# A decoder trunk on one core: seven row tiles of the first gate summed on VectorE, the squares added there, and the norm's steps spread over the last units

## The chip, the cores and the metric

The kernel runs on one core of a Trainium2 chip. The core has TensorE (PE, matrix products, with a queue of its own for loading weights, PEld), VectorE (DVE), ScalarE (ACT), GpSimd (POOL) and SyncE (SP), which issues the transfers that 16 DMA engines carry out. The metric is the device time of one execution in microseconds (us). The kernel before took 1970.44 us, the median of 3 runs (1969.87 to 1972.51).

## What is computed

A trunk of two layers on 256 tokens of width 2048, all in float32. Cut to what matters here:

```
sc = silu(c)
shift_m, scale_m, gate_m, shift_f, scale_f, gate_f = split(sc @ mod_w[0] + mod_b[0], 6)   # six vectors of 2048
h = rmsnorm(x, norm_mix[0]) * (1 + scale_m) + shift_m
x = x + gate_m * pool_mixer(h, pool_w[0], pool_scale[0])          # causal means over 2, 4, 8, 16 tokens, then a product per group
h = rmsnorm(x, norm_ffn[0]) * (1 + scale_f) + shift_f
x = x + gate_f * swiglu(h, ffn_gate[0], ffn_up[0], ffn_down[0])
...                                                               # layer 1: latent attention on shared keys and values, then its own swiglu
return rmsnorm(x, final_norm)
```

Each of the six vectors is a product of one row (sc) with a 2048 x 2048 block of `mod_w`, 16 MB that are read once. The pooling mixer of layer 0 needs the first three vectors, the feed-forward part behind it the next two.

## The kernel before

The front of the kernel (up to the first matrix product of layer 0's feed-forward part) is written in an order by hand: inside `tc.manual_schedule()` each engine executes its instructions in the order in which the code gives them. It is a list of 56 units. Units 0 to 15 stream the weights of `shift_m`, 16 to 31 those of `scale_m`, 32 to 47 those of `gate_m`, one row tile (128 rows x 2048) each, 1 MB; units 48 to 55 (the "block") stream the first 512 columns of `shift_f` and `scale_f`, two row tiles each, also 1 MB. Behind unit n the functions that `then(n, ...)` has put down are called, for one n in the order in which they were put down.

A unit (class `Strips`, line 240) loads its tile into one of six `raw` buffers, through SP's queue, and `use` (line 255) multiplies it on PE: `s_strip` holds silu(c) in the first of 32 columns for each row tile, so that four matmuls of 512 columns write to four strips of 32 partitions of one PSUM bank, over which the units of one vector add up. A float32 matmul is two instructions, so a unit has eight. Behind the last unit of a vector, `columns` (line 265) copies the bank with ACT and turns it with small matmuls (line 273) into columns; `with_bias` (line 783) adds the bias on DVE.

Layer 0's mixer works on turned data, `xT`, 16 tiles of 128 x 256. `pool_modulate` (line 828) applies scale and shift to a group of four tiles (line 832 on ACT, line 834 on DVE), `pool_product` (line 842) computes a quarter of a group on PE and, for each second quarter, copies the result with ACT (line 848). `mix_in` (line 852) adds the gated result to `xT` on DVE (line 856) and squares it on ACT (line 861). `mix_total` (line 864) sums the squares over the 128 partitions with matmuls of one column, 16 instructions per group of four tiles, all into one PSUM tile `total`. `norm_total` (line 878) makes the root mean square from it (line 456 on DVE, line 457 on POOL), spreads it over the partitions by a diagonal matrix (line 884 on DVE) and a matmul (line 886), and copies it to `rstd_b` with ACT (line 887). `turn_back` (line 871) turns a group of `xT` back with eight PE transposes (line 875) and two DVE copies (line 876), for the residual stream. `hidden_T` (line 889) scales a group by `rstd_b` on DVE (line 894), `halves_T` (line 898) applies scale and shift and splits the result in two parts (lines 903 to 905), which the feed-forward part multiplies.

The feed-forward part (line 433) splits each weight tile of 1 MB into two parts, one copied by ACT (line 409), the rest subtracted by DVE (line 411). `w_early` loads and splits its first tile ahead of its turn. Beside it, the vectors of later use are summed in the background on DVE (lines 235 and 293), into accumulators of the tag `acc`, which has two buffers; `front`, the tile that holds `s_strip`, the biases and the gate's columns, is one of these.

In the kernel before, behind unit 31 + g follows `pool_modulate(g)`; behind units 32 to 47 one quarter of the pool product each; behind unit 47 `mix_in` of all four groups; behind unit 48 + g `mix_total(g)`; behind unit 51 + g `turn_back(g)`; behind unit 51 `norm_total`, behind 52 `hidden_T(0)`, behind 53 `w_early`.

Of the kernel before, what the change touches and what calls it, by code (L numbers as in the profile page):

```python
# [17 lines left out]
P = 128  # L18
# [82 lines left out]
def tile_trunk(ctx: ExitStack, tc: tile.TileContext, a: dict, out: bass.AP):  # L101
# [9 lines left out]
    def nm(s):  # L111
        n_names[0] += 1
        return f"{s}_{n_names[0]}"
# [10 lines left out]
    def t2k(shape, dt=F32):  # L124
        return work.tile(shape, dt, tag="t2k", bufs=7, name=nm("t2k"))

    def small(shape, dt=F32, bufs=4):
        return work.tile(shape, dt, tag="sm", bufs=bufs, name=nm("sm"))
# [4 lines left out]
    def ps_t():  # L133
        return psum.tile([P, CH], F32, tag="ps", name=nm("ps"))
# [53 lines left out]
    pool.memset(mhalf, -0.5)  # L188


    front = work.tile([P, KD * (STRIP + 7)], F32, tag="acc", bufs=2, name="front")
    s_strip = front[:, :KD * STRIP].rearrange("p (k m) -> p k m", m=STRIP)
    bcol = front[:, KD * STRIP:KD * (STRIP + 5)].rearrange("p (i k) -> p i k", k=KD)
    gm_col, ps_col = (front[:, KD * (STRIP + i):KD * (STRIP + i + 1)] for i in (5, 6))
    pool.memset(front[:, :KD * STRIP], 0.0)
    cps = ps_t()
    pe.transpose(cps[:, :KD], crow, ident[:KD, :KD])
    s_col = const.tile([P, KD], F32, name="s_col")
# [19 lines left out]
    class Part:  # L218
        def __init__(self, w, b, done):
            self.w, self.b, self.done, self.kt = w, b, done, 0  # L220
# [17 lines left out]


    class Strips:  # L240
        def __init__(self, i, pair, done):
            self.n, self.rows, self.done, self.kt = (2, 2, done, 0) if pair else (NSTRIP, 1, done, 0)
            w = a["mod_w"][0][:, i * D:(i + self.rows) * D]
            self.w = w.rearrange("(k p) (i n) -> p k i n", p=P, i=2)[:, :, :, :CH] if pair else                 w.rearrange("(k p) (i n) -> p k i n", p=P, i=NSTRIP)
# [8 lines left out]
            self.use(self.load())  # L253

        def use(self, r):
            if self.kt == 0:
                self.bank = ps_t()
            for m in range(NSTRIP):
                k, i = m // self.n, m % self.n
                pe.matmul(self.bank[m * STRIP:(m + 1) * STRIP, :], lhsT=s_strip[:, self.kt + k, :], rhs=r[:, k, i, :],  # L260
                          start=self.kt == 0, stop=self.kt + self.rows == KD)
            self.kt += self.rows
            if self.kt == KD:
                self.done(self.columns())

        def columns(self):

# [157 lines left out]
    def w_early(src):  # L425
        early[repr(src)] = w_unit(src)
# [27 lines left out]
    def rsqrt_mean(dst, ss, n):  # L454
        v = small([P, NT])
        dve.tensor_scalar(out=v, in0=ss, scalar1=1.0 / n, scalar2=EPS, op0=ALU.mult, op1=ALU.add)
        pool.tensor_tensor(out=dst, in0=v, in1=mhalf, op=ALU.pow)
# [117 lines left out]
    def ffn_weights(l):  # L575
        return a["ffn_gate"][l], a["ffn_up"][l], a["ffn_down"][l]
# [202 lines left out]
    def with_bias(dst, v, i, factor=None):  # L779

        kt = slice(0, v.shape[1] * KL)
        col = lambda t_: t_[:, kt].rearrange("p (i b) -> p i b", b=KL)
        dve.tensor_tensor(out=col(dst), in0=v, in1=col(bcol[:, i]), op=ALU.add)  # L783
        if factor is not None:
            dve.tensor_tensor(out=col(dst), in0=col(dst), in1=col(factor), op=ALU.mult)
# [4 lines left out]

    shift = Strips(0, False, lambda v: with_bias(cols[:, C_SM0, :], v, 0))
    scale = Strips(1, False, lambda v: with_bias(cols[:, C_AM0, :], v, 1, vcol[:, V_NM:V_NM + KD]))
    gate = Strips(2, False, lambda v: with_bias(gm_col, v, 2, ps_col))
    block = Strips(3, True, block_cols)


# [50 lines left out]
        if n % 2 == 1:  # L847
            act.activation(ysum[g // 2][:, g % 2, n - 1:n + 1, :], mixed[g], AF.Copy)

    squares, total = {}, ps_t()  # L850

    def mix_in(g):

        for k in range(KL):
            kt = g * KL + k
            dve.scalar_tensor_tensor(out=xT[:, kt, :], in0=ysum[g // 2][:, g % 2, k, :], scalar=gm_col[:, kt:kt + 1],
                                     in1=xT[:, kt, :], op0=ALU.mult, op1=ALU.add)
        squares[g] = []
        for h2 in range(2):
            sq = t2k([P, 2, T])  # L860
            act.activation(sq, xT[:, g * KL + 2 * h2:g * KL + 2 * h2 + 2, :], AF.Square)
            squares[g].append(sq)

    def mix_total(g):
        for k in range(KL):
            for tok in range(NT):
                pe.matmul(total[:, tok:tok + 1], lhsT=squares[g][k // 2][:, k % 2, tok * P:(tok + 1) * P], rhs=ones[:, 0:1],
                          start=g + k + tok == 0, stop=g == ND - 1 and k == KL - 1 and tok == NT - 1)


    def turn_back(g):
# [3 lines left out]
                pe.transpose(pt[:, k * P:(k + 1) * P], xT[:, g * KL + k, tok * P:(tok + 1) * P], ident)  # L875
            dve.tensor_copy(back[tok][:, g * CH:(g + 1) * CH], pt)

    def norm_total():

        r = small([P, NT])  # L880
        rsqrt_mean(r, total[:, :NT], D)
        diag = t2k([P, NT, P])
        for tok in range(NT):
            dve.tensor_scalar(out=diag[:, tok, :], in0=ident, scalar1=r[:, tok:tok + 1], scalar2=None, op0=ALU.mult)
        pt = ps_t()
        pe.matmul(pt[:, :T], lhsT=ones, rhs=diag.rearrange("p t q -> p (t q)"), start=True, stop=True)
        act.activation(rstd_b, pt[:, :T], AF.Copy)

    def hidden_T(j):
        parts = []  # L890
        for k in range(KL):
            if k % 2 == 0:
                both = t2k([P, 2, T])
            dve.tensor_tensor(out=both[:, k % 2, :], in0=xT[:, j * KL + k, :], in1=rstd_b, op=ALU.mult)
            parts.append(both[:, k % 2, :])
        return parts
# [14 lines left out]
    def then(n, f, *args):  # L911
        after.setdefault(n, []).append((f, args))
# [7 lines left out]
    then(16, rope_tables)  # L920
    for g in range(ND):
        then(n_mix - 8 + 2 * g, load_pool_w, g)
        then(n_mix - 1 + g, pool_modulate, g)
        for q in range(4):
            then(n_mix + 4 * g + q, pool_product, g, q)
        then(n_block - 1, mix_in, g)
        then(n_block + g, mix_total, g)
        then(n_block + 3 + g, turn_back, g)
    then(n_block + 3, norm_total)
    then(n_block + 4, lambda: first.append(hidden_T(0)))  # L930
    then(n_block + 5, lambda: w_early(ffn_weights(0)[GATE][0:CH, 0:CH]))

    with tc.manual_schedule():
        flat_all = hl_t([P, len(WINDOWS), T], F32)
        pool_all = [act_t([P, 2, KL, T], F32) for _ in range(2)]
        back = [t_.rearrange("p g k t -> p (g k t)") for t_ in pool_all]
        stat_start()
        for tok in range(NT):
            for j in range(ND):
                stat_piece(tok, j, xn[tok])  # L940
        rstd = stat_finish()
        for n, part in enumerate(units):
            if n < len(ahead):
                part.use(ahead[n])
            else:
                part.unit()
            for f, args in after.get(n, ()):
                f(*args)
        first = halves_T(0, first[0])
# [302 lines left out]
```

## Time and profile before

| | |
|---|---|
| median of 3 runs | 1970.44 us (1969.87 to 1972.51) |
| the profiled execution | 1972.76 us, span from first to last instruction 1971.0 us |
| busy share of the span | PE 96%, PEld 78%, DVE 73%, ACT 43%, POOL 2% |
| mean granted TensorE clock | 0.978 of full speed |
| first matmul of the feed-forward part (line 433) | 192.01 us after the span's start |

All times in the profile count from the span's start. A row of the timeline merges neighbouring instructions of one line: start, duration, engine, line, operation, out<-in, count, and in brackets how long the engine was idle before it and what ended this. TensorE's clock is either full (2.4 GHz, shown as 1.00) or half (1.2 GHz, 0.50); a value between is a stretch in which it changed.

### The profile page before, as it was taken

To read this page: it belongs to the slowest core of one execution; us is meant where nothing else is said; L and a number is where in the kernel's file an instruction comes from. 1 tells how busy PE (TensorE), PEld (TensorE's weight loads), DVE (VectorE), ACT (ScalarE), POOL (GpSimd) and SP (SyncE) were. 2 spreads that over 40 slices of the span, in tenths; PEclk is the share of its full clock that TensorE was granted. 3 is DMA by queue.
4 is the path that set the end of the run, shared out by engine and by line. 5 is a ranking of instruction groups with operands and counts; after the bars stand their busy time and mean duration, and the time that the engine had idled before them with its cause. 6 is when DMAs were issued, how large, how long until landed. Compare 5 with 4: busy or idle time off the path is not lost. (4 is left out here: it accounts for less than half of the span.)

```text
span 1971.0 us, 22348 instructions
## 1 busy us (share of the span) xinstructions
PE 1895.6 (96%) x8949; PEld 1532.0 (78%) x8949; DVE 1442.2 (73%) x1298; ACT 843.0 (43%) x915; POOL 30.1 (2%) x30
## 2 busy tenths in 40 slices
PE   6698999999999999999899999999999999999998
PEld 3145788888888888887788987888888888888886
DVE  1114989999778778888989985889987556554556
ACT  3023444444533333334675744544444433343333
POOL 0000000000000000000000000000000000000000
PEclk9787999999999999999899999999999999999999
DMA  9997999998998989988788684989977667665661
GB/s 395 412 404 277 350 342 336 316 322 314 341 335 299 329 311 332 335 332 313 277 317 308 217 306 136 355 304 325 313 279 259 231 235 256 235 203 187 195 221 70
DMA packets 225441, 572.73 MB, mean 291 GB/s; under 512 B 11997, under 2 KB 16421, under 8 KB 203571
## 3 DMA queue, kind: packets, MB, share of 16 engines
q1 hardware_dynamic: 225338, 571.31, 81.1%
q8 instruction: 70, 1.15, 0.2%
q14 instruction: 33, 0.27, 0.0%
HBM read 564.98 MB, written 6.29 MB: 290 GB/s over the span
## 5 line engine op out<-in xcount | busy, mean ns | idle before, releaser
L433 PE MATMUL ps<-hl,act 128*128 128x512 f32 x7008 | 1610.9, 391 | 6.2 <-ACT hl L409 2.7
L433 PEld LDWEIGHTS ps<-hl,act 128*128 128x128 f32 x7008 | 1317.1, 189 | 282.1 <-ACT hl L409 3.6
L411 DVE TENSOR_TENSOR hl<-raw,hl 128x2048 fp32r<-128x2048 f32 x296 | 676.3, 2288 | 244.1 <-ACT hl L409 239.8
L409 ACT ACTIVATE hl<-raw 128x2048 fp32r<-128x2048 f32 x296 | 566.5, 1917 | 666.3 <-PE ps L433 595.0
L235 DVE SCALAR_TENSOR_TENSOR acc<-raw,s_col,acc 128x2048 f32<-128x2048 f32 x112 | 262.6, 2345 | 1.2 <-DMA raw<-in_mod_w_dram 1.0
L293 DVE SCALAR_TENSOR_TENSOR acc<-raw,s_col,acc 128x1024 f32<-128x1024 f32 x112 | 143.3, 1279 | 2.1 <-DMA raw<-in_mod_w_dram 0.8
L260 PE MATMUL ps<-raw,front 128*32 128x512 f32 x448 | 74.0, 749 | 26.3 <-DMA raw<-in_mod_w_dram 26.2
L600 DVE TENSOR_TENSOR act<-ps,act 128x512 f32<-128x512 f32 x96 | 64.0, 685 | 10.6 <-PE ps L433 10.3
L260 PEld LDWEIGHTS ps<-raw,front 128*32 128x32 f32 x448 | 10.4, 121 | 61.2 <-DMA raw<-in_mod_w_dram 46.3
L669 DVE TENSOR_TENSOR x<-ps,x 128x512 f32<-128x512 f32 x32 | 22.1, 690 | 33.6 <-PE ps L433 33.6
L634 ACT ACTIVATE act<-ps 128x512 fp32r<-128x512 f32 x44 | 23.6, 593 | 40.0 <-PE ps L631 36.6
L452 ACT ACTIVATE junk<-x 128x512 bf16<-128x512 f32 x24 | 15.1, 628 | 59.9 <-DVE x L550 39.7
L678 ACT ACTIVATE t2k<-ps 128x512 f32<-128x512 f32 x24 | 14.2, 591 | 56.6 <-PE ps L433 56.6
L1050 PE MATMUL ps<-act,hl 128*128 128x256 f32 x128 | 37.2, 291 | 0.5 <-DVE hl L411 0.5
L845 PEld LDWEIGHTS ps<-act,act 128*128 128x128 f32 x128 | 24.1, 198 | 16.3 <-issue 12.6
L1051 PE MATMUL ps<-act,hl 128*128 128x256 f32 x128 | 36.7, 287 | 0.0
L783 DVE TENSOR_TENSOR cols<-ps,front 128x16 f32<-128x16 f32 (+1 forms) x4 | 0.6, 166 | 49.3 <-PE ps L273 49.2
L1052 PE MATMUL ps<-act,hl 128*128 128x256 f32 x128 | 36.1, 286 | 0.0
L682 DVE TENSOR_TENSOR t2k<-ps,t2k 128x512 f32<-128x512 f32 x24 | 16.6, 690 | 25.7 <-PE ps L433 25.7
L845 PE MATMUL ps<-act,act 128*128 128x256 f32 x128 | 33.7, 408 | 0.0
L598 ACT ACTIVATE act<-ps 128x512 f32<-128x512 f32 x32 | 19.0, 596 | 26.9 <-PE ps L433 26.8
L500 ACT ACTIVATE t2k<-ps,cols 128x256 f32<-128x256 f32 x48 | 24.8, 569 | 12.4 <-PE ps L486 11.8
(188 smaller groups left out, 981.6 us busy)
## 6 DMA issues: line engine op xcount, KB each, us to landing
raw<-in_mod_w_dram SPq DMA_DIRECT2D x128, 1024.0 KB, 7.3
raw<-in_ffn_gate_dram SPq DMA_DIRECT2D x88, 1024.0 KB, 7.3
raw<-in_ffn_up_dram SPq DMA_DIRECT2D x88, 1024.0 KB, 5.2
raw<-in_ffn_down_dram SPq DMA_DIRECT2D x88, 1024.0 KB, 5.2
raw<-in_mod_w_dram SPq DMA_DIRECT2D x128, 512.0 KB, 5.8
raw<-in_kv_mod_w_dram SPq DMA_DIRECT2D x32, 1024.0 KB, 7.1
raw<-in_w_o_dram SPq DMA_DIRECT2D x16, 1024.0 KB, 5.2
raw<-in_w_uq_dram SPq DMA_DIRECT2D x8, 768.0 KB, 6.3
```

The costliest lines, as they stand in the source:

```text
L235: dve.scalar_tensor_tensor(out=self.acc, in0=r, scalar=s_col[:, self.kt:self.kt + 1], in1=self.acc, op0=ALU.mult, op1=ALU.add)
L260: pe.matmul(self.bank[m * STRIP:(m + 1) * STRIP, :], lhsT=s_strip[:, self.kt + k, :], rhs=r[:, k, i, :], start=self.kt == 0, stop=self.kt ...
L293: dve.scalar_tensor_tensor(out=self.acc, in0=r[:, k], scalar=s_col[:, self.kt + k:self.kt + k + 1], in1=self.acc, op0=ALU.mult, op1=ALU.add)
L409: hi_ins = act.activation(hi, r, AF.Copy)
L411: lo_ins = dve.tensor_tensor(out=lo, in0=r, in1=hi.bitcast(F32), op=ALU.subtract)
L433: pe.matmul(banks[tok], lhsT=t_[:, i, k, tok * P:(tok + 1) * P], rhs=w[:, k, :], start=first and n < len(part), stop=last and n >= len(ord ...
L500: act.activation(full, pts[k // 2][:, k % 2, :], AF.Identity, scale=scale, bias=bias)
L600: dve.tensor_tensor(out=part, in0=banks[tok], in1=part, op=ALU.add)
L845: pe.matmul(mixed[g][:, n % 2, :], lhsT=wp[g][:, k, ns], rhs=pool_all[g // 2][:, g % 2, k, :], start=k == 0, stop=k == KL - 1)
L1050: pe.matmul(pt[:, h, :], lhsT=wl(h0 + h, k), rhs=t_[:, 0, k, :], start=k == 0, stop=False)
L1051: pe.matmul(pt[:, h, :], lhsT=wh(h0 + h, k), rhs=t_[:, 0, k, :], start=False, stop=False)
L1052: pe.matmul(pt[:, h, :], lhsT=wh(h0 + h, k), rhs=t_[:, 1, k, :], start=False, stop=k == KL - 1)
```

## The change

Units 32, 34, 36, 38, 40, 42 and 44, the even row tiles 0 to 12 of the gate, are multiplied by silu(c) and summed on DVE into an accumulator of the tag `acc` in place of PE's strips. Behind the strips of unit 47, the accumulator goes through the strips once, with a column of ones in place of silu(c). `pool_modulate` of groups 1 to 3 moves to units 33, 36 and 39, each quarter of the pool product by one unit (33 to 48). `mix_in` of groups 0 to 2 stays behind unit 47, that of group 3 goes behind unit 48. The squares are added on DVE over the row tiles, an add one half group behind its square, into one tile of two rows of tiles; `norm_sums` behind unit 51 sums it over the partitions with four matmuls and makes the diagonal. `turn_back(g)` moves to unit 49 + g, the spread of the norm and `hidden_T(0)` to unit 53, `w_early` to unit 52. Four tiles of the norm are allocated ahead of unit 47.

```diff
+    front = work.tile([P, KD * (STRIP + 7) + STRIP], F32, tag="acc", bufs=2, name="front")
+    one_strip = front[:, KD * (STRIP + 7):]
...
+    pool.memset(one_strip, 0.0)
+    pool.memset(one_strip[:, 0:1], 1.0)
...
         def use(self, r):
-            if self.kt == 0:
+            last = self.kt + self.rows == KD
+            if self.kt in self.aside:
+                s_ = s_col[:, self.kt:self.kt + 1]
+                if self.acc is None:
+                    self.acc = work.tile([P, 1, NSTRIP, CH], F32, tag="acc", bufs=2, name=nm("acc"))
+                    dve.tensor_scalar(out=self.acc, in0=r, scalar1=s_, scalar2=None, op0=ALU.mult)
+                else:
+                    dve.scalar_tensor_tensor(out=self.acc, in0=r, scalar=s_, in1=self.acc, op0=ALU.mult, op1=ALU.add)
+            else:
+                self.sum(lambda k: s_strip[:, self.kt + k, :], r, last and self.acc is None)
+            if last and self.acc is not None:
+                self.sum(lambda k: one_strip, self.acc, True)
+            self.kt += self.rows
+            if self.kt == KD:
+                self.done(self.columns())
+
+        def sum(self, weights, r, last):
+            first = self.bank is None
+            if first:
                 self.bank = ps_t()
             for m in range(NSTRIP):
                 k, i = m // self.n, m % self.n
-                pe.matmul(self.bank[m * STRIP:(m + 1) * STRIP, :], lhsT=s_strip[:, self.kt + k, :], rhs=r[:, k, i, :],
-                          start=self.kt == 0, stop=self.kt + self.rows == KD)
-            self.kt += self.rows
-            if self.kt == KD:
-                self.done(self.columns())
+                pe.matmul(self.bank[m * STRIP:(m + 1) * STRIP, :], lhsT=weights(k), rhs=r[:, k, i, :], start=first, stop=last)
...
-    gate = Strips(2, False, lambda v: with_bias(gm_col, v, 2, ps_col))
+    gate = Strips(2, False, lambda v: with_bias(gm_col, v, 2, ps_col), range(0, KD - 2, 2))
...
     def mix_in(g):
 
-        for k in range(KL):
-            kt = g * KL + k
-            dve.scalar_tensor_tensor(out=xT[:, kt, :], in0=ysum[g // 2][:, g % 2, k, :], scalar=gm_col[:, kt:kt + 1],
-                                     in1=xT[:, kt, :], op0=ALU.mult, op1=ALU.add)
-        squares[g] = []
         for h2 in range(2):
-            sq = t2k([P, 2, T])
-            act.activation(sq, xT[:, g * KL + 2 * h2:g * KL + 2 * h2 + 2, :], AF.Square)
-            squares[g].append(sq)
-
-    def mix_total(g):
-        for k in range(KL):
-            for tok in range(NT):
-                pe.matmul(total[:, tok:tok + 1], lhsT=squares[g][k // 2][:, k % 2, tok * P:(tok + 1) * P], rhs=ones[:, 0:1],
-                          start=g + k + tok == 0, stop=g == ND - 1 and k == KL - 1 and tok == NT - 1)
+            for k in range(2 * h2, 2 * h2 + 2):
+                kt = g * KL + k
+                dve.scalar_tensor_tensor(out=xT[:, kt, :], in0=ysum[g // 2][:, g % 2, k, :], scalar=gm_col[:, kt:kt + 1],
+                                         in1=xT[:, kt, :], op0=ALU.mult, op1=ALU.add)
+            pair = xT[:, g * KL + 2 * h2:g * KL + 2 * h2 + 2, :]
+            if g + h2 == 0:
+                act.activation(squares, pair, AF.Square)
+            else:
+                sq = t2k([P, 2, T])
+                act.activation(sq, pair, AF.Square)
+                late.append(lambda sq=sq: dve.tensor_tensor(out=squares, in0=squares, in1=sq, op=ALU.add))
+                if len(late) > 1:
+                    late.pop(0)()
+
+    late = []
+
+    def norm_sums():
+        late.pop()()
+        for tok in range(NT):
+            for k in range(2):
+                pe.matmul(total[:, tok:tok + 1], lhsT=squares[:, k, tok * P:(tok + 1) * P], rhs=ones[:, 0:1],
+                          start=tok + k == 0, stop=tok + k == 2)
+        rsqrt_mean(rstd_x1, total[:, :NT], D)
+        for tok in range(NT):
+            dve.tensor_scalar(out=diag[:, tok, :], in0=ident, scalar1=rstd_x1[:, tok:tok + 1], scalar2=None, op0=ALU.mult)
...
+    def norm_spread():
+
+        pe.matmul(total[:, T:], lhsT=ones, rhs=diag.rearrange("p t q -> p (t q)"), start=True, stop=True)
+        act.activation(rstd_b, total[:, T:], AF.Copy)
...
-        then(n_mix - 1 + g, pool_modulate, g)
+        then(n_mix - 1 + 3 * g - (g > 0), pool_modulate, g)
         for q in range(4):
-            then(n_mix + 4 * g + q, pool_product, g, q)
-        then(n_block - 1, mix_in, g)
-        then(n_block + g, mix_total, g)
-        then(n_block + 3 + g, turn_back, g)
-    then(n_block + 3, norm_total)
-    then(n_block + 4, lambda: first.append(hidden_T(0)))
-    then(n_block + 5, lambda: w_early(ffn_weights(0)[GATE][0:CH, 0:CH]))
+            then(n_mix + 1 + 4 * g + q, pool_product, g, q)
+        then(n_block - (g < ND - 1), mix_in, g)
+        then(n_block + 1 + g, turn_back, g)
+    then(n_block + 3, norm_sums)
+    then(n_block + 5, norm_spread)
+    then(n_block + 5, lambda: first.append(hidden_T(0)))
+    then(n_block + 4, lambda: w_early(ffn_weights(0)[GATE][0:CH, 0:CH]))
...
+            if n == n_block - 1:
+                squares, diag, total, rstd_x1 = t2k([P, 2, T]), t2k([P, NT, P]), ps_t(), small([P, NT])
```

## Rows read from the trace of the kernel before

**Rows 1.** The page's first part: busy us, share of the span, instructions.

```profile
PE 1895.6 (96%) x8949; PEld 1532.0 (78%) x8949; DVE 1442.2 (73%) x1298; ACT 843.0 (43%) x915; POOL 30.1 (2%) x30
```

**Rows 2.** Windows of 10 us: busy of each engine, granted clock, DMA share, GB/s.

```profile
120.00:130.00 10.00, 10.00 (x58) 5.17 (x58) 1.50 (x4) 2.17 (x5) 0.00 (x0) 1.00 1.01 416
...
150.00:160.00 10.00, 9.28 (x56) 5.68 (x56) 2.00 (x7) 1.83 (x3) 0.00 (x0) 1.00 1.01 360
...
210.00:220.00 10.00, 10.00 (x46) 8.26 (x45) 9.96 (x8) 6.01 (x6) 0.53 (x1) 1.00 0.98 336
```

**Rows 3.** Timeline of 100 to 135, PE: the gate's units.

```profile
104.05 1.93 PE L260 MATMUL ps<-raw,front 128*32 128x512 f32 x8 [3.23 <-DMA raw<-in_mod_w_dram]
...
110.36 3.78 PE L845 MATMUL ps<-act,act 128*128 128x256 f32 x8
...
120.01 1.07 PE L260 MATMUL ps<-raw,front 128*32 128x512 f32 x8
...
121.00 1.99 PE L845 MATMUL ps<-act,act 128*128 128x256 f32 x8
...
122.93 1.07 PE L260 MATMUL ps<-raw,front 128*32 128x512 f32 x8
```

**Rows 4.** Timeline of 155 to 182: the gate's end, mixing and the norm.

```profile
155.05 1.07 PE L260 MATMUL ps<-raw,front 128*32 128x512 f32 x8
...
158.14 0.18 DVE L785 TENSOR_TENSOR front<-front 128x16 f32<-128x16 f32 x1
158.35 5.63 DVE L856 SCALAR_TENSOR_TENSOR x<-act,front,x 128x256 f32<-128x256 f32 x14
...
172.55 1.97 PE L875 MATMUL ps<-con,x 128*128 128x128 f32 x8
...
177.76 0.16 DVE L456 TENSOR_SCALAR sm<-ps 128x2 f32<-128x2 f32 x1 [2.51 <-PE ps L867]
...
178.74 0.48 DVE L884 TENSOR_SCALAR t2k<-con,sm 128x128 f32<-128x128 f32 x2 [0.82 <-POOL sm L457]
...
179.37 1.19 PE L886 MATMUL ps<-t2k,ones 128*128 128x256 f32 x2 [1.64 <-DVE t2k L884]
...
180.49 1.94 PE L260 MATMUL ps<-raw,front 128*32 128x512 f32 x8
```

**Rows 5.** Timeline of 182 to 215: the front's end.

```profile
183.15 1.29 DVE L876 COPY act<-ps 128x512 f32<-128x512 f32 x2 [3.92 <-PE ps L875]
...
184.35 1.42 DVE L894 TENSOR_TENSOR t2k<-x,krT 128x256 f32<-128x256 f32 x4
...
186.49 1.09 PE L875 MATMUL ps<-con,x 128*128 128x128 f32 x8
...
186.89 2.28 DVE L411 TENSOR_TENSOR hl<-raw,hl 128x2048 fp32r<-128x2048 f32 x1
...
187.51 1.06 PE L260 MATMUL ps<-raw,front 128*32 128x512 f32 x8
...
192.01 0.73 PE L433 MATMUL ps<-hl,act 128*128 128x512 f32 x2 [1.60 <-ACT act L904]
```

**Rows 6.** Groups by line, 100 to 196: count, busy us, mean ns, idle before.

```profile
L867 PE MATMUL ps<-ones,t2k 128*128 128x1 f32 x64 | 10.9, 300 | 0.0
...
L834 DVE SCALAR_TENSOR_TENSOR act<-act,cols,t2k 128x256 f32<-128x256 f32 x16 | 6.5, 479 | 6.0 <-ACT t2k L832 5.9
```

**Rows 7.** Windows of 1 us in which the clock changed.

```profile
165.00:166.00 1.00, 1.00 (x9) 0.53 (x12) 0.31 (x1) 0.57 (x1) 0.00 (x0) 0.76 1.05 377
...
182.00:183.00 1.00, 1.00 (x9) 0.65 (x6) 0.00 (x0) 0.78 (x1) 0.00 (x0) 0.70 0.00 0
```

**Rows 8.** The page's parts 5 and 6: VectorE's sums; the units' loads.

```profile
L235 DVE SCALAR_TENSOR_TENSOR acc<-raw,s_col,acc 128x2048 f32<-128x2048 f32 x112 | 262.6, 2345 | 1.2 <-DMA raw<-in_mod_w_dram 1.0
...
raw<-in_mod_w_dram SPq DMA_DIRECT2D x128, 1024.0 KB, 7.3
```

**Rows 9.** The chain that ended last: start, us, engine, line.

```profile
1962.55 0.70 DVE x L550
```

More of the change, by code (lines that the diff above doesn't have):

```diff
@@ L188, in tile_trunk @@
     pool.memset(mhalf, -0.5)
-    front = work.tile([P, KD * (STRIP + 7)], F32, tag="acc", bufs=2, name="front")
+    front = work.tile([P, KD * (STRIP + 7) + STRIP], F32, tag="acc", bufs=2, name="front")
     s_strip = front[:, :KD * STRIP].rearrange("p (k m) -> p k m", m=STRIP)
+    one_strip = front[:, KD * (STRIP + 7):]
     bcol = front[:, KD * STRIP:KD * (STRIP + 5)].rearrange("p (i k) -> p i k", k=KD)
@@ L240, in tile_trunk, with __init__ @@
     class Strips:
-        def __init__(self, i, pair, done):
+        def __init__(self, i, pair, done, aside=()):
+            self.aside, self.acc, self.bank = aside, None, None
             self.n, self.rows, self.done, self.kt = (2, 2, done, 0) if pair else (NSTRIP, 1, done, 0)
@@ L848, in pool_product @@
             act.activation(ysum[g // 2][:, g % 2, n - 1:n + 1, :], mixed[g], AF.Copy)
-    squares, total = {}, ps_t()
     def mix_in(g):
-        for k in range(KL):
-            kt = g * KL + k
-            dve.scalar_tensor_tensor(out=xT[:, kt, :], in0=ysum[g // 2][:, g % 2, k, :], scalar=gm_col[:, kt:kt + 1],
-                                     in1=xT[:, kt, :], op0=ALU.mult, op1=ALU.add)
-        squares[g] = []
-        for h2 in range(2):
-            sq = t2k([P, 2, T])
-            act.activation(sq, xT[:, g * KL + 2 * h2:g * KL + 2 * h2 + 2, :], AF.Square)
-            squares[g].append(sq)
-    def mix_total(g):
-        for k in range(KL):
-            for tok in range(NT):
-                pe.matmul(total[:, tok:tok + 1], lhsT=squares[g][k // 2][:, k % 2, tok * P:(tok + 1) * P], rhs=ones[:, 0:1],
-                          start=g + k + tok == 0, stop=g == ND - 1 and k == KL - 1 and tok == NT - 1)
+        for h2 in range(2):
+            for k in range(2 * h2, 2 * h2 + 2):
[21 more added lines that the diff above has]
+            dve.tensor_scalar(out=diag[:, tok, :], in0=ident, scalar1=rstd_x1[:, tok:tok + 1], scalar2=None, op0=ALU.mult)
     def turn_back(g):
@@ L876, in turn_back @@
             dve.tensor_copy(back[tok][:, g * CH:(g + 1) * CH], pt)
[L878 to L887, printed above, removed]
+    def norm_spread():
+        pe.matmul(total[:, T:], lhsT=ones, rhs=diag.rearrange("p t q -> p (t q)"), start=True, stop=True)
+        act.activation(rstd_b, total[:, T:], AF.Copy)
     def hidden_T(j):
```

## The prediction, put down before the kernel was run

> **What bounds the kernel now.** TensorE (PE) is busy for 96% of the span [rows 1], and in the feed-forward part it is full: 46 matmuls of 512 columns in 10 us, 10.00 us busy at 210:220 [rows 2]. So the time after the first of these matmuls (line 433, at 192.01 [rows 5]) is taken as fixed, and the change is worth what it moves that start by. Before it lies the front: 56 units of 1 MB each that SP loads into six `raw` buffers.
>
> I read three views of the front. The windows first: at 120:130 the DMA moves 416 GB/s at a full share, so a unit (1.049 MB) lands every 2.52 us; at 150:160, with the block's smaller pieces, 360 GB/s [rows 2], between 2.8 and 2.9 us a unit. The PE timeline of the gate's units next: strips start at 120.01 and again at 122.93 [rows 3]. That is 2.92 us a unit, 0.40 more than the load: a quarter of the pool product (1.99) and the strips (1.07) overlap only slightly. PE is the bound there, and the buffers fill. Unit 31 is used at 104.05 as it lands [rows 3]; at the load's pace unit 47 would land at 104.05 + 16 x 2.52 = 144.4, but its strips start at 155.05 [rows 4]. Last the tail: from the end of those strips (156.1) to line 433 it takes 35.9 us. The row sums of the squares alone take 10.9 us of PE (64 instructions, line 867 [rows 6]), then PE waits for the norm chain (177.76 to 179.37 [rows 4]), all at a clock that had fallen from full to half in 165:166 and came back in 182:183 [rows 7]. So the front has two places where PE, not the load, decides.
>
> **The change part by part.**
>
> *Gate on VectorE (DVE).* Units 32, 34, ... 44 no longer issue strips; one more pass over the accumulator is added at unit 47. PE per pair of units becomes 2 x 1.98 + 0.94 (a strip pass beside a quarter, 2.92 - 1.98) = 4.9 us against 5.04 for two loads: balanced. Working: unit 33 lands at 109.1; its strips at half clock take 1.93 (at 104.05 [rows 3]), the quarter 3.78 (at 110.36 [rows 3]), to 114.8. Then 13 quarters (units 34 to 46), 13 x 1.98 = 25.7; eight strip passes (35, 37, 39, 41, 43, 45, 46, 47), 7.5; the pass over the accumulator 1.0. End: 149.0, 7.1 us earlier than 156.1. PE stays 2 to 4 us behind the loads and so never idle.
>
> DVE pays seven passes over 128x2048. Six are of a form that the trace has: 2.35 us [rows 8]. The first is a product with one tensor operand, which the trace lacks at this size: between 0.24 (the 128x128 one, half of 0.48 at 178.74 [rows 4]) and 2.35; I take 2.35, the row of its size. Together 16.4 us, with 5 us of pool modulation (of 6.5 [rows 6]) in the 37 us from 112 to 149: DVE was idle there, and is filled to 58%. The last sum (unit 44, landed at 136.8) is done near 140, nine before it is read. The buffer of such a unit is freed by DVE; at most 5 us after landing, when a modulation stands ahead of it. A load takes 7.3 us [rows 8] and the sixth next unit lands 15 later, so 8 us are spare. The two memsets more on the strip of ones lie at the start on POOL, hidden by the first loads.
>
> The modulations of groups 1 to 3 move from units 32, 33, 34 to 33, 36, 39, and each quarter by one unit: group 1 is first read at unit 37, group 3 at 45. At nothing; if that cover were gone, PE would wait for four modulations, 1.6 us a group.
>
> *Squares added on DVE, one sum at the end.* The 64 row-sum instructions (10.9 us) become 8, by the same rows 1.0 at full, 1.8 at half clock. ACT's squares stay. DVE pays seven adds of 128x512; nearest rows: 0.70 for one at this size [rows 9], and twice 0.355 from four of 128x256 in 1.42 at 184.35 [rows 5]. I take 0.62, between; both ends move the sum by 0.6.
>
> *The tail, in order.* The column chain stays as long as it was (156.1 to 158.3 [rows 4]): the gate column is ready at 151.2. PE then does the last two quarters, strips 48 to 51 and three groups of turning back (1.0 each at full, 186.49 [rows 5]), and is done at 161.5. Now DVE is late: the sum at unit 51 waits for its last add, and ahead of that in DVE's order stand 16 mixes (5.63 for 14, 6.5 [rows 4]), seven adds (4.3) and the six copies of three groups (1.29 for two [rows 5], 3.9): 14.7 us, from 151.2 to 165.9. Behind the waiting sum stand PE's strips of unit 52, and behind these the release of buffers. So 4.4 us of PE idle is the new wait. PSUM has room: the sum's, the block's and six turning banks are eight.
>
> From 165.9: row sums 1.8 (half clock), to 167.7; strips 52 to 169.6; turning group 3 to 171.5; then I let the clock be full again, as it came back in 182:183 behind the spread matmul and a unit's strips [rows 4, 7]; strips 53 to 172.5; spread matmul 0.65 (1.19 at half [rows 4]) to 173.1. It does not wait: line 456 to the diagonal's end took 1.5 us [rows 4], so the diagonal is ready at 169.2. Strips 54 and 55 to 175.1. From the end of strips 55 (188.6) to line 433 (192.01) it was 3.45 [rows 5]: 178.5. **Gain 13.5 us.**
>
> Beside it: DVE copies group 3 by 172.9, splits the first weights (now ahead of the scaling, 2.28) by 175.2, scales the first hidden tile (1.42) by 176.6 [rows 5], before the block's columns need it at 177.0. The early weight load is issued one unit earlier; unit 55 lands at 144.4 + 8 x 2.85 + 2.5 = 169.7, before 174.1. So the load is hidden, with 4 us to spare.
>
> SP: the accumulator of the first background part now gets the gate's buffer, so its memset on POOL, which could run at the start, waits until 149 or behind the norm's power at 168; its bias load, and the loads of two further tiles, stand behind it in SP's queue. The up-projection's buffer comes free only with strips 52 (169.6), so this costs below 1 us; I take 0.
>
> *Clock.* In 165:166 the clock fell to 0.76, half from there [rows 7], while PE was issuing one-column row sums without a pause. So the full look of PE in the timeline doesn't keep the clock, and a PE that waits 4.4 us and then issues such sums will hardly do so. The Trainium skill ("TensorE: Matmul & The Clock Gate", section "HAM oscillation — how this bites in real kernels") says that a wait for data puts the clock down and that the next burst begins cold. By that rule the wait which replaces the row sums costs what they did in clock, and the time is that of the forecast or of the first rival; by the row alone, read as a fault of one-column matmuls, the second rival's. That the trace has a fall beside a PE shown as busy is more than the rule says; it speaks for the fall here too.
>
> **Rivals.**
> 1. *Half clock to the end.* Strips at 1.93, turning 1.97, spread 1.19 [rows 3, 4]; the column matmuls, eight as in a strip pass, taken as longer by the same 0.85: sums 167.7, then 169.6, 171.5, 173.4, 174.6, 176.5, 178.4, and 4.3 to line 433: 182.7, gain 9.3, 1961.1 us. For it: it held half over 17 us before. Against: then one-column sums filled most of it, now 128-column turning does.
> 2. *Full clock.* Sums 166.95, 167.9, 168.9, 169.85, 170.5, 171.4, 172.4, plus 3.45: 175.9, gain 16.1, 1954.3 us. Even with PE at no cost the loads give 169.7 + 1.0 + 3.45 = 174.2, gain 17.8, 1952.6.
> 3. *Gate units no faster*, because a buffer held by DVE or a late modulation stalls PE as long as the strips did: only the tail's 6.4 remain, 1964.0 us. Against: DVE's idle time there.
> 4. *The next loads wait.* If the background accumulator gets the front's buffer instead, free at 178, SP stands until 179; two loads of 7.3 us and a split (4.2) come at 191, PE has used the first weights by 184.5: 6.5 lost, and the DMA's idle 11 us are missed later, where it is full. Gain 2 to 7, about 1966.5.
> 5. *DVE becomes the bound: slower.* Its added 16.4 + 4.3 = 20.7 us all fall on the path, against 5.7 (six strip passes) and 9.5 saved on PE: +5.5, 1975.9 us. It decides once DVE lags a landing by more than the 8 us that the buffers spare, so that loads stop for it. Against: 58%.
>
> **How the numbers follow.** The profiled execution took 1972.76 us (span 1971.0 and 1.76 around it); less 13.5 that is 1959.3. The median of the runs is 2.3 lower, so 1970.44 - 13.5 = 1956.9 us. Chances: forecast 0.45, rival 1 0.17, rival 2 0.14, rival 3 0.09, rival 4 0.08, rival 5 0.07. The range 1952.5 to 1964.5 holds forecast, rivals 1 and 2 and most of 3. A measurement of this kernel tells 0.2% (3.9 us) from no change: faster is below 1966.5. Forecast, rivals 1 to 3 and a third of rival 4 make 0.88; 0.05 is left for the same, 0.07 for slower.
>
> **What would show it.** Strips of unit 47 ending at 149 with PE full from 115; DVE near 58% there. A PE wait of 4 to 5 us before the row sums, released by an add on DVE, and half clock behind it. First line 433 at 178.5. Later pace as before: 46 matmuls in 10 us. Wrong if PE waits for DVE within the gate's units, if line 433 starts on time but then waits for weights, or if strips 55 wait for their load.

## The result, and the profile after

The changed kernel takes 1956.78 us, the median of four runs (1954.77 to 1956.92), against 1970.47 before: 13.7 us less, ratio 0.9926 with the interval 0.9909 to 0.9944 (11 to 18 us). The forecast was 1956.9. A second timing, beside the kernel before, gave 0.9925 (0.9911 to 0.9938).

The profiled execution took 1956.75 us. Page, first lines (busy us, share, instructions):

```profile
span 1954.6 us, 22168 instructions
...
PE 1875.0 (96%) x8845; PEld 1519.7 (78%) x8845; DVE 1461.5 (75%) x1312; ACT 843.9 (43%) x915; POOL 30.4 (2%) x32
```

PE issues 104 instructions fewer than in [rows 1]: 56 one-column sums and 48 of the gate's strips. The lines have new numbers in the changed kernel: the strips of line 260 are at L282, the quarters of line 845 at L864, and the first matmul of the feed-forward part, still called line 433 here, is at L451. The gate's units, in the timeline of the changed kernel (start, us, engine, line, operation, out<-in, count):

```profile
108.75 1.93 PE L282 MATMUL ps<-raw,front 128*32 128x512 f32 x8 [0.54 <-DMA raw<-in_mod_w_dram]
...
110.34 1.28 DVE L265 TENSOR_SCALAR acc<-raw,s_col 128x2048 f32<-128x2048 f32 x1
...
110.61 4.47 PE L864 MATMUL ps<-act,act 128*128 128x256 f32 x16
...
113.12 2.34 DVE L267 SCALAR_TENSOR_TENSOR acc<-raw,s_col,acc 128x2048 f32<-128x2048 f32 x1
...
115.02 1.07 PE L282 MATMUL ps<-raw,front 128*32 128x512 f32 x8
...
116.01 3.72 PE L864 MATMUL ps<-act,act 128*128 128x256 f32 x16
...
119.67 1.06 PE L282 MATMUL ps<-raw,front 128*32 128x512 f32 x8
...
138.73 1.06 PE L282 MATMUL ps<-raw,front 128*32 128x512 f32 x8 [0.27 <-DMA raw<-in_mod_w_dram]
...
145.45 1.04 PE L282 MATMUL ps<-acc,front 128*32 128x512 f32 x8
...
146.59 0.95 POOL L304 MEMSET acc<- 128x1024 f32 x1 [127.96 <-PE ps L282]
```

Read against [rows 3]: one strip pass and two quarters, from 115.02 to 119.67, now make 4.65 us for two units where each unit took 2.92. At 138.73 the strips wait 0.27 us for their load: PE has caught up. The pass over the accumulator ends at 146.49; in [rows 4] the strips of unit 47 ended at 156.12. The memset of the next accumulator follows at once, at 146.59.

The tail, from the timeline of 148 to 186, and three windows of 1 us in which the clock changed (third column from the right):

```profile
157.99 1.09 PE L903 MATMUL ps<-con,x 128*128 128x128 f32 x8
...
158.72 3.68 DVE L904 COPY act<-ps 128x512 f32<-128x512 f32 x6
...
162.31 0.69 DVE L882 TENSOR_TENSOR t2k<-t2k,t2k 128x512 f32<-128x512 f32 x1
...
163.06 1.60 PE L892 MATMUL ps<-ones,t2k 128*128 128x1 f32 x8 [3.98 <-DVE t2k L882]
...
164.59 1.93 PE L282 MATMUL ps<-raw,front 128*32 128x512 f32 x8
...
166.45 1.97 PE L903 MATMUL ps<-con,x 128*128 128x128 f32 x8
...
168.35 1.94 PE L282 MATMUL ps<-raw,front 128*32 128x512 f32 x8
...
170.22 0.70 PE L908 MATMUL ps<-t2k,ones 128*128 128x256 f32 x2
...
170.85 1.92 PE L282 MATMUL ps<-raw,front 128*32 128x512 f32 x16
...
176.20 0.74 PE L451 MATMUL ps<-hl,act 128*128 128x512 f32 x2 [1.60 <-ACT act L926]
```

```profile
112.00:113.00 1.00, 1.00 (x6) 0.84 (x5) 1.00 (x4) 0.00 (x0) 0.00 (x0) 0.91 0.97 393
...
163.00:164.00 1.00, 0.94 (x6) 0.94 (x6) 0.00 (x1) 0.00 (x0) 0.00 (x0) 0.69 1.05 387
...
170.00:171.00 1.00, 1.00 (x10) 0.45 (x10) 1.00 (x1) 0.05 (x1) 0.00 (x0) 0.90 1.05 395
```

PE ends the turning of group 2 at 159.08 and waits 3.98 us for the last add of squares (162.31 on DVE), which stands behind six copies (158.72, 3.68 us). The clock goes to half just behind that wait, at about 163.4, and stays there to about 170.2 (worked out from the shares in 163:164 and 170:171): the strips at 164.59 and 168.35 take 1.93 and 1.94 us, those at 170.85 1.92 for two units. Line 433 starts at 176.20, 15.8 us before [rows 5]. Behind it little changed: from line 433 to the end of the span it is 1778.4 us, against 1779.0 before, and in the fourteen profiles of this study between 1776.8 and 1779.1.

### The profile page after: what moved, and what is told of

Read it like the earlier page. It is cut to its first block, busy times and chain, and to the rows that moved or that the text cites. A ratio compares the mean times of both kernels' runs of the same rounds, so it can differ in the third digit from the quotient of the medians.

```text
span 1954.6 us, 22168 instructions
## 1 busy us (share of the span) xinstructions
PE 1875.0 (96%) x8845; PEld 1519.7 (78%) x8845; DVE 1461.5 (75%) x1312; ACT 843.9 (43%) x915; POOL 30.4 (2%) x32
## 5 line engine op out<-in xcount | busy, mean ns | idle before, releaser
L451 PE MATMUL ps<-hl,act 128*128 128x512 f32 x7008 | 1610.0, 391 | 5.7 <-ACT hl L427 2.1
L451 PEld LDWEIGHTS ps<-hl,act 128*128 128x128 f32 x7008 | 1315.6, 188 | 282.2 <-ACT act L926 3.2
L282 PE MATMUL ps<-raw,front 128*32 128x512 f32 x392 | 64.8, 752 | 27.6 <-DMA raw<-in_mod_w_dram 27.5
L282 PEld LDWEIGHTS ps<-raw,front 128*32 128x32 f32 x392 | 9.3, 120 | 60.2 <-DMA raw<-in_mod_w_dram 48.0
L1076 PE MATMUL ps<-act,hl 128*128 128x256 f32 x128 | 35.9, 283 | 0.0
L864 PEld LDWEIGHTS ps<-act,act 128*128 128x128 f32 x128 | 24.1, 194 | 11.4 <-issue 8.4
L864 PE MATMUL ps<-act,act 128*128 128x256 f32 x128 | 31.0, 394 | 0.0
L616 ACT ACTIVATE act<-ps 128x512 f32<-128x512 f32 x32 | 19.0, 596 | 27.2 <-PE ps L451 27.1
```

What stands on the lines that cost most here:

```text
L282: pe.matmul(self.bank[m * STRIP:(m + 1) * STRIP, :], lhsT=weights(k), rhs=r[:, k, i, :], start=first, stop=last)
L451: pe.matmul(banks[tok], lhsT=t_[:, i, k, tok * P:(tok + 1) * P], rhs=w[:, k, :], start=first and n < len(part), stop=last and n >= len(ord ...
L864: pe.matmul(mixed[g][:, n % 2, :], lhsT=wp[g][:, k, ns], rhs=pool_all[g // 2][:, g % 2, k, :], start=k == 0, stop=k == KL - 1)
L1076: pe.matmul(pt[:, h, :], lhsT=wh(h0 + h, k), rhs=t_[:, 1, k, :], start=False, stop=k == KL - 1)
```

## The experiments

All are compared with the kernel before. "Tail" is the stretch from the end of the gate's last strips (or of the pass over the accumulator) to line 433. One window over it gives PE's busy time, DVE's, and the mean granted clock; the half-clock time is twice (1 - clock) times its length.

**The kernel before, profiled again.** No edit.

> The kernel before, unchanged, profiled a second time. Its first profiled execution took 1972.76 us, 2.3 above the median of its runs, and the profiled gain was 16.0 us where the medians differ by 13.7. Theory A: that execution met TensorE's clock changes at an unlucky moment of the front, so a second one takes about 1970.4, with the first line-433 matmul 1.5 to 3 us earlier than 192.01 (at 189 to 190.5) or with less half clock behind it. Theory B: the 2.3 us lie in the long feed-forward part or around the span, and line 433 starts at 192.0 again, within 0.3.

Line 433 started at 192.25, and the span was 1969.4: theory B holds. Of the 2.3 us by which the first profiled execution lay above the median, 1.9 lie behind line 433 (1779.0 against 1777.2). The two tails:

```profile
156.12:192.01 35.89, 31.16 (x187) 20.12 (x187) 16.52 (x38) 9.87 (x16) 1.65 (x2) 0.76 0.72 242
```

```profile
154.78:192.25 37.47, 32.74 (x186) 21.66 (x187) 16.53 (x38) 9.86 (x16) 1.65 (x2) 0.73 0.69 237
```

35.9 us at a mean clock of 0.76, and 37.5 at 0.73: 17.2 and 20.2 us of half clock.

**The changed kernel, profiled again.** No edit.

> The changed kernel, unchanged, profiled a second time. First profile: strips of unit 47 and the pass over the accumulator end at 146.5, line 433 starts at 176.20, 1956.75 us. If the place of the clock's changes is all that differs between executions, the gate's end lies between 145.5 and 148.5 and line 433 between 174.5 and 178.5, and the wait for the last add of squares is 3.5 to 4.5 us again, since VectorE's chain behind the gate's column does not depend on TensorE's clock.

The gate's end was at 146.9, the wait 3.98 us again, line 433 at 175.77, 1955.6 us: all as expected. The tails of the two profiles:

```profile
146.49:176.20 29.71, 22.64 (x139) 12.13 (x138) 20.70 (x45) 10.10 (x16) 2.61 (x3) 0.89 1.04 376
```

```profile
146.93:175.77 28.84, 21.77 (x139) 12.26 (x138) 20.50 (x45) 10.09 (x16) 2.60 (x3) 0.87 1.04 379
```

6.5 and 7.5 us of half clock.

**The gate's part alone.** The kernel before with the class `Strips`, the strip of ones, and these lines of the change:

```diff
+    gate = Strips(2, False, lambda v: with_bias(gm_col, v, 2, ps_col), range(0, KD - 2, 2))
+        then(n_mix - 1 + 3 * g - (g > 0), pool_modulate, g)
+            then(n_mix + 1 + 4 * g + q, pool_product, g, q)
+        then(n_block - (g < ND - 1), mix_in, g)
```

> Only the gate's part of the change (seven row tiles on VectorE, modulation and quarters moved); squares, their 64 one-column row sums, norm and turning back as in the kernel before. Theory of the prediction, parts add: the gate's strips end at 146.5 as in the changed kernel (9.6 earlier than 156.1) and the tail from there to line 433 stays 35.9, so line 433 at 182.4 and a gain of 7 to 10 us, 1961 to 1963.5 by the median. Rival, the load bounds the front behind the gate: the earlier end is mostly waited off and the tail grows to 40 or more, gain below 5 us.

1959.36 us, 12.3 less than before (ratio 0.9942, 0.9928 to 0.9955), more than expected. The gate's end came at 146.7 as forecast, but the tail shrank too:

```profile
146.66:180.41 33.75, 29.02 (x196) 18.63 (x195) 16.52 (x38) 9.98 (x16) 2.60 (x3) 0.90 0.96 343
```

The same 64 one-column sums as before, but a quarter of the pool product now stands between the first two groups of them, and half clock falls to 6.8 us. That this quarter is the reason is argued: no run moved it alone.

**The tail's part alone.** The changed kernel with these lines back:

```diff
+    gate = Strips(2, False, lambda v: with_bias(gm_col, v, 2, ps_col))
+        then(n_mix - 1 + g, pool_modulate, g)
+            then(n_mix + 4 * g + q, pool_product, g, q)
```

> Only the tail's part of the change (squares added on VectorE, one row sum, norm and turning back spread); the gate's 16 units on TensorE, modulation and quarters where they were. Parts add: gate's end at 156.1, tail 29.7 as in the changed kernel, line 433 at 185.8, gain 5 to 7 us, 1963.5 to 1965.5 by the median. Rival, both parts remove the same wait (the load's): the tail falls to 25 and the gain is over 10 us.

1964.09 us, 7.6 less (0.9963, 0.9950 to 0.9975). The tail is 28.9 us, as short as in the changed kernel, with a longer wait of PE for the same add:

```profile
155.03:183.95 28.92, 19.79 (x133) 11.00 (x131) 20.58 (x45) 9.98 (x16) 1.65 (x2) 0.87 0.85 292
```

```profile
171.60 1.87 PE L892 MATMUL ps<-ones,t2k 128*128 128x1 f32 x8 [6.04 <-DVE t2k L882]
```

The parts do not add: 12.3 + 7.6 = 19.9, and together they gave 13.7 to 14.1 by the medians (16.1 by the one execution, 1955.60, that was timed beside these two runs). By line 433, it is 11.6 and 8.1 us alone and 15.8 together. They share a saving, which is the long half clock: it is 17 to 20 us with neither part, 7 with either one and 7 with both. If half of it is lost time, about 5 us are counted twice in the sum; line 433 shows 3.9.

**PE kept at work through the wait, with wide work.**

```diff
     def norm_sums():
+        for _ in range(29):
+            pe.transpose(total[:, P:2 * P], ident, ident)
         late.pop()()
```

> The changed kernel, with 29 transposes of 128 columns (of a constant, into an unused part of the norm's bank) put on TensorE ahead of the one row sum, so that the engine works through the 4.0 us in which it waited for the last add of squares. They change no result. Theory A, the wait itself is hidden and only the half clock behind it (163.2 to 170.2) is on the path: the row sum starts at 163.0 to 163.6 as before, the clock stays at 1.00, line 433 starts at 172.8 to 174, 2 to 3.4 us earlier than 176.20, gain over the changed kernel 2 to 3.4 us. Rival B, the load bounds the last units: strips of unit 55 wait for their load and line 433 moves by less than 1 us. Rival C, the clock falls all the same: line 433 within 0.7 of 176.2.

1953.07 us (0.9906, 0.9892 to 0.9921). Theory A:

```profile
158.86 3.33 PE L890 MATMUL ps<-con 128*128 128x128 f32 x29
163.00 1.05 PE L894 MATMUL ps<-ones,t2k 128*128 128x1 f32 x8 [0.81 <-DVE t2k L882]
163.98 1.07 PE L282 MATMUL ps<-raw,front 128*32 128x512 f32 x8
...
172.98 16.60 PE L451 MATMUL ps<-hl,act 128*128 128x512 f32 x63 [1.60 <-ACT act L928]
```

```profile
146.43:172.98 26.55, 22.64 (x169) 13.96 (x168) 20.51 (x45) 10.11 (x16) 2.61 (x3) 1.00 1.05 386
```

The row sums start when they did (163.00), and at a clock of 1.00 line 433 comes 3.2 us earlier. At this order of loads the wait as such cost nothing; the clock behind it did.

**The same with one-column work.**

```diff
     def norm_sums():
+        for _ in range(16):
+            pe.matmul(total[:, P:P + 1], lhsT=ident, rhs=ones[:, 0:1], start=True, stop=True)
         late.pop()()
```

> As the run before it, but with 16 one-column float32 matmuls (32 instructions, 4 us at the row sums' 0.12 us each) in place of the transposes: TensorE is shown busy all the same, but moves one column each. If the clock falls only where the engine is idle, it stays at 1.00 and line 433 starts at 172.8 to 174. If one-column work does not hold it, as the kernel before suggests (fall at 165.5 while such sums ran without a pause), the clock falls between 160 and 165 and line 433 starts at 175.5 to 178, as in the changed kernel.

1956.31 us (0.9921, 0.9906 to 0.9936), line 433 at 176.31, as in the changed kernel:

```profile
159.66 4.54 PE L890 MATMUL ps<-ones,con 128*128 128x1 f32 x32
164.06 1.85 PE L894 MATMUL ps<-ones,t2k 128*128 128x1 f32 x8
165.83 1.93 PE L282 MATMUL ps<-raw,front 128*32 128x512 f32 x8
```

```profile
160.00:162.00 2.00, 2.00 (x20) 2.00 (x19) 2.00 (x5) 1.91 (x1) 0.00 (x0) 1.00 1.04 385
162.00:164.00 2.00, 2.00 (x12) 2.00 (x12) 1.74 (x3) 0.00 (x0) 0.00 (x0) 0.54 1.05 388
...
168.00:170.00 2.00, 2.00 (x16) 1.31 (x14) 1.15 (x2) 0.00 (x0) 0.00 (x0) 0.75 1.00 293
```

PE is busy without a gap from 159.66 to 164.06, and the clock is at 0.54 in 162:164. Half clock lasts from about 162.2 to 169.0, as long as behind the wait in the changed kernel. Here a PE that is shown as busy with one-column matmuls lost its clock as the one that waited.

**The turning-back copies on ScalarE.**

```diff
     def turn_back(g):
...
-            dve.tensor_copy(back[tok][:, g * CH:(g + 1) * CH], pt)
+            act.activation(back[tok][:, g * CH:(g + 1) * CH], pt, AF.Copy)
```

> The changed kernel, with the copies of turning back on ScalarE instead of VectorE. VectorE's chain behind the gate's column loses six copies (3.7 us): if that chain is what ends the wait, the row sum starts at 159.5 to 160 instead of 163.06, TensorE waits under 1 us there, the clock stays up, and the last units run at the load's pace: strips of unit 55 at 168 to 169, line 433 at 172.3 to 173.5, gain over the changed kernel 2.7 to 4 us. Rival, the wait only moves (to the diagonal, to the first weights' split or to ScalarE's queue): line 433 at 175 or later.

1952.84 us (0.9906, 0.9891 to 0.9920), as expected:

```profile
160.37 1.05 PE L892 MATMUL ps<-ones,t2k 128*128 128x1 f32 x8 [0.64 <-DVE t2k L882]
...
167.36 1.05 PE L282 MATMUL ps<-raw,front 128*32 128x512 f32 x4 [0.30 <-DMA raw<-in_mod_w_dram]
168.71 1.05 PE L282 MATMUL ps<-raw,front 128*32 128x512 f32 x4 [0.30 <-DMA raw<-in_mod_w_dram]
...
173.17 42.12 PE L451 MATMUL ps<-hl,act 128*128 128x512 f32 x171 [1.60 <-ACT act L926]
```

The row sums wait 0.64 us instead of 3.98, the clock stays up, and strips of the last units wait for their loads (0.30 us twice). So DVE's six copies set the wait, and the load is what comes next.

**All but the last two row tiles on VectorE.**

```diff
+    gate = Strips(2, False, lambda v: with_bias(gm_col, v, 2, ps_col), range(KD - 2))
```

> The changed kernel with 14 row tiles of the gate on VectorE instead of 7. VectorE then has 14 sums (1.3 + 13 x 2.35 = 31.8 us) and three modulations (5.0) from 110.3 on, so it ends at 147 or later, and the pass over the accumulator waits for it. If VectorE becomes the bound from there, gate's end at 148 to 150 instead of 146.5, TensorE waiting on an add of line 267, and the kernel 1.5 to 4 us slower than the changed one. Rival, TensorE is still the bound of the gate's units and fewer strips help: gate's end at 145.5 or earlier, 1 us faster.

1956.69 us, no slower than the changed kernel; half a miss. The gate's end came later, as expected:

```profile
132.94 14.28 DVE L267 SCALAR_TENSOR_TENSOR acc<-raw,s_col,acc 128x2048 f32<-128x2048 f32 x6
...
141.38 1.94 PE L282 MATMUL ps<-raw,front 128*32 128x512 f32 x8 [6.69 <-DMA raw<-in_mod_w_dram]
...
147.38 1.06 PE L282 MATMUL ps<-acc,front 128*32 128x512 f32 x8 [0.18 <-DVE acc L267]
```

The pass over the accumulator waits for DVE (0.18), whose last sum ended at 147.22, and ends at 148.44, 1.9 later than in the changed kernel. DVE was not alone in this. PE had run out of work and waited 6.69 us for the load of unit 46, which came at the load's own pace (unit 31 at 103.89, and 15 x 2.52 us later is 141.7); its strips then ran at half clock, and those of unit 47 ended only at 147.19, just before DVE. Line 433 came at 176.54 all the same: the tail is 28.1 us, 1.6 shorter than in the changed kernel's first profile, at a clock of 0.93. That is 3.9 us of half clock against 6.5, and half of the difference, as an estimate, 1.3 of the 1.6 us. One profile does not tell whether another execution would repeat it.

**The kernel before, with more work on PE.**

```diff
     def mix_total(g):
...
+        pt = ps_t()
+        for _ in range(8):
+            pe.transpose(pt[:, :P], ident, ident)
```

> The kernel before, with eight more transposes of 128 columns of a constant (1.1 us at full clock) behind each group's 16 one-column row sums, four groups; they change no result and only add work to TensorE, 4.3 us. In the two profiles of the kernel before, the tail from the gate's end to line 433 holds 17.1 and 20.5 us of half clock. Theory A, one-column sums let the clock fall and the fall costs half of that time, 8 to 10 us, on the path: with the wider work between them the half clock shrinks to 7 us or less, the tail to 31 to 34 us (from 35.9 and 37.5), and a kernel with more work is 2 to 6 us faster than the one before. Rival B, the clock is a by-product of waits that stand there anyway: the tail grows by the added 4 us and the kernel is 2 to 4 us slower.

1966.26 us, 5.2 less than before (0.9974, 0.9964 to 0.9984), with 4.3 us more work:

```profile
155.10:186.61 31.51, 27.71 (x219) 18.81 (x218) 16.43 (x38) 9.86 (x16) 1.65 (x2) 1.00 0.83 282
```

The clock is 1.00 through the whole tail, which shrinks from 35.9 and 37.5 to 31.5. So in the kernel before the half clock was no by-product of waits. The tail less the added 4.3 us is 27.2; the two profiles of the kernel before are 8.7 and 10.3 us above that, about half of their 17.2 and 20.2 us of half clock. That the one-column sums, more than the strips between them, let it fall is argued here; the one-column fill above shows it for the changed kernel.

**The first weights' load behind unit 55, besides ScalarE's copies.**

```diff
-    then(n_block + 4, lambda: w_early(ffn_weights(0)[GATE][0:CH, 0:CH]))
+    then(n_block + 7, lambda: w_early(ffn_weights(0)[GATE][0:CH, 0:CH]))
```

> The changed kernel with the turning-back copies on ScalarE (as in the run where line 433 started at 173.17 and strips 54 and 55 waited 0.30 us each for their loads), and the early load of the first feed-forward weights and its split moved from behind unit 52 to behind unit 55, so that unit 55's load is one transfer (2.7 us) nearer. If the load is the bound there, strips of unit 55 come 1.5 to 2.5 us earlier, line 433 starts at 171 to 172, a gain of 1 to 2 us over that run. Rival, the weights' own load, now last, and its split (1.9 on ScalarE, 2.3 on VectorE, ahead of the first hidden tile's parts) decide: line 433 at 173 or later, or a wait of TensorE behind its first matmuls, and no gain.

1950.91 us (0.9898, 0.9883 to 0.9913), 20.6 less than before. The last strips run from 164.28 without a wait of note, and line 433 starts at 170.91, held for 2.72 us by ScalarE, where the weights' split now stands ahead of the hidden tile's parts and itself waited 0.92 us for their load. That is 2.3 us earlier than in the run with ScalarE's copies alone:

```profile
164.28 2.10 PE L282 MATMUL ps<-raw,front 128*32 128x512 f32 x16
...
168.01 1.91 ACT L427 ACTIVATE hl<-raw 128x2048 fp32r<-128x2048 f32 x1 [0.92 <-DMA raw<-in_ffn_gate_dram]
...
170.91 44.39 PE L451 MATMUL ps<-hl,act 128*128 128x512 f32 x182 [2.72 <-ACT act L926]
```

**Both once more, timed side by side.** No edits.

> The changed kernel again, timed beside the kernel before and beside the version with ScalarE's copies and the late weight load. The three profiles so far put line 433 at 192.0 and 192.3 before, 176.2 and 175.8 after, and 1776.8 to 1779.0 us behind it in every kernel. So the gain by fast runs is 14 to 16.5 us, more than the 13.7 of the first comparison, if line 433 is what decides; near 13 if the feed-forward part gives some of it back.

> The version with ScalarE's copies and the first weights' load behind unit 55, a second time, now in one call with the changed kernel. Line 433 was at 170.91 there, 5 us before the changed kernel's; if that carries through, it is 4 to 6.5 us faster than the changed kernel on the same chip.

1956.23 us for the changed kernel (14.1 less than before, 0.9925), 1951.23 for the other (0.9900, 0.9887 to 0.9914): 5.0 us apart, with line 433 at 176.37 and 171.38. The version with both edits beats the changed kernel. The 14.1 is at the low end of what was expected: line 433 came nearly 16 us earlier again, and part of this does not show in the medians.

## Why the prediction was right, and where its terms were off

*What bounds the kernel.* Right. Line 433 decides, and the rest kept its length within 2.3 us in fourteen profiles. Against line 433 the forecast gain of 13.5 us was too small by 2.3 (15.8 in the first pair of profiles, 16.5 in the second); against the medians (13.7 and 14.1) it was not. That the median came within 0.2 us of the forecast is partly luck: line 433 came 2.3 us before the forecast's 178.5, and the first medians show 2.1 us less than line 433 does. By as much the part behind it differs between executions (1776.8 to 1779.1); no run tells why.

*Gate on VectorE: the term that was mis-sized.* The gate's end was forecast for 149.0 and came at 146.5. Of these 2.5 us, 1.8 lie ahead of the strips of unit 35, which the working puts at 116.8 and which started at 115.02. Unit 33's strips started 0.35 earlier than assumed, and the first two quarters took 4.47 us instead of 5.76, since the clock came back in 112:113 and not at 114.8. The forecast had taken the 3.78 us of one profile [rows 3] as fixed; in the second profile of the same kernel that quarter took 2.57:

```profile
110.33 2.57 PE L845 MATMUL ps<-act,act 128*128 128x256 f32 x8
```

So that part is chance: in the other profiles with seven tiles on DVE the first two quarters took 4.23 to 5.54 us, and the gate ended between 146.4 and 147.5.

The other 0.7 us are the pairs of units. PE's pair costs 4.65 us, not 4.9: two quarters back to back take 3.72 together, 1.86 each, where no strip pass stands between them. But the five pairs from 115.02 to 138.73 took 23.7 us, not 23.25, as PE met the load. "PE never idle" was slightly wrong: it waited for the load at 138.73.

DVE's part held. Its share of 110 to 150 was 55%, with sums at 2.34 us. The first product took 1.28, half of what I took and within its bounds. The Trainium skill ("VectorE: DVE Perf Modes", section "Mode 2×_2P — use both read ports for one tensor") says that a float32 operation with one tensor operand in SBUF can use both read ports and goes twice as fast as one with two; 1.28 against 2.34 agrees.

*Tail.* Forecast 29.5 us from the gate's end to line 433, measured 29.7 and 28.8. The wait was forecast as 4.4 us and is 3.98; DVE's chain, forecast as 14.7 us, ran from 148.7 to 163.0, 14.3. The half clock was let run to 22.5 us behind the gate's end; it lasted to 23.7, through the strips of unit 53 too (168.35), which cost back about what DVE's shorter chain and the shorter sums gave. With the clock held (the wide fill) the tail is 26.6 us. Rival 2 put that at 26.9, and the forecast's difference between the two cases, 2.6 us, was 3.2.

What the forecast did not separate is why the tail gained its 6.2 us. Taking half of the half-clock time off each tail as an estimate of it at full clock gives 35.9 - 8.6 = 27.3 for the kernel before (27.4 in its second profile) and 29.7 - 3.3 = 26.4 after (25.1 in its second). The runs with wide transposes, at a clock of 1.00, measured nearly this: 31.5 - 4.3 = 27.2 for the kernel before and 26.6 after. So of the 6.2 us some 5 are clock (6 of 8.6 by the second profiles). Of the 6.8 us of PE's work that the squares on DVE removed, most came back: about 1.9 as a second quarter of the pool product that now stands behind the gate's end, and 2.3 as idle time of PE, 4.7 us before and 7.1 after, where the wait for DVE's chain stands. I had counted the sums' 10.9 us as work removed, all at half clock; but in the kernel before two of the four groups ran at full:

```profile
163.52 1.95 PE L867 MATMUL ps<-ones,t2k 128*128 128x1 f32 x16
...
167.18 3.58 PE L867 MATMUL ps<-ones,t2k 128*128 128x1 f32 x16
```

At full clock they are 7.8 us of work, four groups at 1.95 (as three groups in the gate-only run show too), and the half clock lay on the strips and matmuls beside them as well.

*The clock.* The fall came behind the wait, as forecast. The reading of [rows 7] behind it was loose: the clock fell at about 165.5, where PE passed from the second group of sums (to 165.47) to strips, so PE had done sums and strips in turn, not sums alone. The Trainium skill ("TensorE: Matmul & The Clock Gate", section "HAM oscillation — how this bites in real kernels") says that a wait for data puts the clock down and that the next burst begins cold. The trace agrees for the wait of 3.98 us, with half clock from 0.3 us behind its end; in the one-column fill PE lost its clock without a wait, and there the measurement decides.

*Rivals.* Half clock to the end did not happen: full clock came back after 6.8 us, in which PE did sums, strips and turning without a pause. The gate's units were faster, against rival 3. The next accumulator got the gate's buffer, its memset ran at 146.59, and the DMA's share stays near 1.0 from there to line 433 (1.04 over the tail), so no load waited for it, against rival 4 (and earlier than the forecast's worse case of 168). DVE at 55% was no bound of the gate's units, against rival 5; with 14 tiles on it the gate ended 1.9 us later, and the kernel was no slower.

## What to carry to other kernels

Work it out by stage: which engine, load or chain releases the next step, and what comes second. Here each step removed uncovered the next a few microseconds later (strips, row sums, VectorE's copies, the load). In a stretch where TensorE sets the pace, look at the granted clock as well as at what the work costs. Here one-column matmuls, and a wait of 4 us for another engine, were paid a second time by the work that followed at half clock, and 3 to 4 us of 128-column transposes put beside them or into the wait made a kernel with more instructions 3 to 5 us faster. Two parts of a change that remove the same hidden cost do not add. And a clock that comes back at different moments in two profiles of one kernel is no fixed term of a sum: take it from more than one profile.

## What was not expected of the hardware

One-column matmuls issued without a gap let the clock fall to half (0.54 in 162:164 with PE busy all the time), while 128-column transposes in the same place held it at 1.00. Adding 4.3 us of such transposes to the kernel before made it 5.2 us faster. The eight matmul instructions of 256 columns of a quarter take 1.99 us between strip passes and 1.86 back to back.
